# Second branch's output matrix as seven block products over all twelve K tiles, product by product, with half of the layer norm kept on chip

## The chip, the cores and the metric

The kernel runs on one core of one Trainium2 chip. The engines meant below are TensorE (PE: matmuls into PSUM; PEld is its weight load), VectorE (DVE), ScalarE (ACT), GpSimd (POOL, which here issues transfers that add into their target) and SyncE (SP, which issues plain loads and stores). Each engine works through its own list of instructions in the order of the program and waits for the others by semaphores. The metric is the time of one execution in microseconds; the median of three runs is given, lower is better.

## The reference, cut to what matters

Everything is float32; batch 1, 1024 positions, model width 1024. The part around the change:

```python
u = va * jax.nn.sigmoid(ga)
u = causal_depthwise_conv(u, conv_a_w[l], conv_a_b[l])
u = jax.nn.silu(layer_norm(u, ln_g[l], ln_b[l]))          # over 1024 channels
y_a = jnp.einsum("bsc,cd->bsd", u, w_a_out[l])            # K = 1024 = 8 tiles of 128

v = causal_depthwise_conv(xb, conv_b_w[l], conv_b_b[l])
v = rg_lru(v, w_rg_a[l], b_rg_a[l], w_rg_x[l], b_rg_x[l], lam[l])
y_b = jnp.einsum("bsc,cd->bsd", v * jax.nn.gelu(gb), w_b_out[l])   # K = 1536 = 12 tiles of 128

m = jax.nn.sigmoid(sa) * y_a + jax.nn.sigmoid(sb) * y_b
x = x + jnp.einsum("bsc,cd->bsd", m, w_o[l])
```

Ahead of it stand an RMS norm and the input projection z, behind it the MLP and two more norms. The change touches y_b and the layer norm.

## The kernel before

**Arithmetic.** A float32 matmul is made of three in the float32r type, with each factor split into a high and a low part: high by high, high by low, low by high. The high part is a copy by ACT; the low part (the factor less its high part) is made either by DVE or by `split_dma`: ACT writes the negative of the rounded value, a POOL transfer adds the factor to it, ACT writes the high part. A matmul multiplies one 128x128 tile of weights or activations with one of 128x512. Large matrix products use Strassen's scheme in Winograd's form: two by two blocks, seven block products (1 to 7) instead of eight, with sums of blocks ahead of them (s1 to s4 on the weights' side, t1 to t4 on the other) and sums of products behind them.

**Order.** The stages around the change lie in `manual_schedule`: the order on each engine is the one in which the Python code issues it. Small tables (`ZX`, `BX`, `GX`) say which preparations come after which product; `at` keeps a rough clock for each engine, and `later`, `vector_work` and the norm's generator use that clock to choose where DVE's work is put in. Buffers come from pools: 37 tiles of 128x1024 (`T`), 7 more (`W`, weights3), 15 of 128x512 (`EV`, evac3), eight PSUM banks of 128x512 (`bank`). A tile that takes a used buffer waits for that buffer's last reader; if it is a load, SP waits, and all of SP's list behind it.

**Branch b.** The gated recurrence's output lies in DRAM as `hgd`, 12 tiles of 128x1024 (channels x positions). y_b has four pairs of output tiles, i = 0 to 3. For each pair, K tiles 4, 5, 10 and 11 go through the seven products (`b_mm` with "1" to "7", 6 matmuls each), and the other eight K tiles through four plain blocks ("00", "01", "10", "11", 24 matmuls each), which add to the same banks. The weights come in two arrays, `w_b_pl` (8 x 512 KB) and `w_b_sq` (4 x 512 KB); their parts are made by ACT and DVE (`b_split`). The order is pair by pair (`bseq`). `b_post` and `b_out` multiply each finished 128x512 block by its gate sb and store it to DRAM (`mbd`).

**Layer norm.** The convolved branch a lies in DRAM as `yd`, 8 tiles. Its two halves over positions are o = 0 and 1. One generator (`n_all`) does the statistics of half 1, then of half 0, then scales both. `n_stats` subtracts the mean, squares (ACT), adds, and sums over channels by two matmuls with a constant matrix, so that the variance stands in a PSUM bank (var), the same in all 128 rows. Half 1's tiles (yc) are stored back to yd after the mean is off and loaded again for the scaling. 1/sigma is one root and a Newton step on 128x512 numbers (lv, lsd, lr: a reciprocal and four more rows on DVE).

**Behind it** comes the stage g: y_a with the same seven products, product by product (`GORD`) and i = 0 to 3 within a product, where ga1h, ga1l and so on are parts of the normed tiles q, and wa tiles are loads of w_a_out; then the product with w_o.

Of the kernel before, what the change touches and what calls it, by code (L numbers as in the profile page):

```python
# [9 lines left out]
F32 = mybir.dt.float32  # L10
# [20 lines left out]
def trunk_kernel(ctx: ExitStack, tc: tile.TileContext, x, xt_in, xt_eo, vecs, w_in, w_a_out, w_b_pl, w_b_sq,  # L31
# [1003 lines left out]

    ZX = {0: ((x_parts, 1, 7),), 2: ((x_parts, 1, 5),), 4: ((x_parts, 1, 4),)}
    H_AT = {2: (0, 0), 5: (1, 1), 3: (0, 1), 4: (1, 0)}
    with tc.manual_schedule(engines=ENGINES):

        hg, hraw, hb_, hbo, wraw_, wop = {}, {}, {}, {}, {}, {}  # L1040

        def hg_load(*ts):
            for t in ts:
                hraw[t] = T(f"hg{t}")
                nc.sync.dma_start(hraw[t], hgd[t])

        def b_split(a, name, mk, mk2=None):
            h, l = mk(name + "h", F32R), (mk2 or mk)(name + "l", F32R)
            nc.scalar.activation(h, a, AF.Copy)
            later(at("A", 1.0), 1.2, nc.vector.tensor_tensor, l, a, h.bitcast(F32), ALU.subtract)  # L1050
            return h, l

        def hg_parts(*ts):
            for t in ts:
                hg[t] = b_split(hraw.pop(t), f"hg{t}", X1 if t == 9 else T)

        def hb_load(kk, hf):
            hb_[kk, hf] = a = T(f"hb{kk}{hf}")
            for c in range(2):
                nc.sync.dma_start(a[:, HALVES[c]], hgd[4 + c + 6 * kk, :, HALVES[hf]])  # L1060

        def hb_t(*ns):

            if 2 in ns:
                hb_[2] = T("hbt2")
            for n in ns:
                o, a, b = {1: ((0, 0), (0, 1), (0, 0)), 2: (2, (1, 1), (0, 0)),
                           3: ((0, 1), (1, 1), (0, 1)), 4: ((1, 0), (1, 0), 2)}[n]
                later(0, 1.2, nc.vector.tensor_tensor, hb_[o], hb_[a], hb_[b], ALU.subtract)

        def hb_parts(p):
            b = {1: (0, 0), 5: (0, 0), 2: (1, 0), 4: (1, 0), 3: (1, 1), 7: (0, 1), 6: 2}[p]
            hbo[p] = b_split(hb_[b], f"hb{p}", T)

        def a_load(i):
            if i < 4:
                wraw_[i, "a"] = a = (W if i else T)(f"wba{i}")
                nc.sync.dma_start(a, w_b_sq[i])

        def a_sums(i):  # L1080
            if i < 4:
                a, s = wraw_[i, "a"], T(f"wbs{i}")
                wraw_[i, "s"] = s
                a11, a12, a21, a22 = (a[:, n * 2 * P:(n + 1) * 2 * P] for n in range(4))
                s1, s2, s3, s4 = (s[:, n * 2 * P:(n + 1) * 2 * P] for n in range(4))
                for o, x, y, op_ in ((s1, a21, a22, ALU.add), (s2, s1, a11, ALU.subtract),
                                     (s3, a11, a21, ALU.subtract), (s4, a12, s2, ALU.subtract)):
                    later(0, 0.4, nc.vector.tensor_tensor, o, x, y, op_)

        def a_parts(i, x):  # L1090
            if i < 4:
                wop[i, x] = b_split(wraw_.pop((i, x)), f"wb{x}{i}", T, W if i and x == "a" else T)

        def p_load(j):
            if j < 8:
                wraw_[j, "p"] = a = (W if j else T)(f"wbp{j}")
                nc.sync.dma_start(a, w_b_pl[j])

        def p_parts(j):
            if j < 8:  # L1100
                wop[j, "p"] = b_split(wraw_.pop((j, "p")), f"wbp{j}", W if j else T)
# [16 lines left out]
        def b_mm(i, x):  # L1118
            if len(x) == 1:
                p = int(x)  # L1120
                b = {1: "b", 2: "a", 3: "e", 4: "b", 5: "e", 6: "b", 7: "f"}[p]
                if p in (1, 7):
                    yb_[i, b] = bank(f"yb{i}{b}")
# [1171 lines left out]
```

## Time and profile before

| | |
|---|---|
| Median of 3 runs | 1528.11 us (1528.05 to 1528.63) |
| Profiled execution | 1528.49 us, span of the records 1526.7 us |
| Branch-b stage, first matmul to the first of stage g | 624.20 to 751.24 us |
| PE, DVE, ACT, POOL busy over the span | 99%, 79%, 61%, 12% |
| Granted TensorE clock | 0.999 |

A row of the profile's timeline gives start and length in us, engine, source line, operation, output tile and input tiles, partitions x elements, a count if rows were put together, and in brackets the idle time before it with what ended that. Lengths of neighbours on one engine overlap, so the cost of one in a row of many is the distance from start to start. PE busy at 99% says that some matmul was always under way.

### The profile page before, as it was taken

The page shows a single profiled execution, that of the slowest core. Times are in us where ns is not written, and L with a number is a line of the kernel's source. Part 1 is how long each engine was busy: PE and PEld are TensorE (multiplying, and loading weights), DVE is VectorE, ACT ScalarE, POOL GpSimd, SP SyncE. Part 2 cuts the span into 40 slices and gives each one's busy share as a digit, 9 for nine tenths or more (in the row PEclk, how much of TensorE's full clock was granted, in tenths as well). Part 3 has the DMA queues.
Part 4 walks back from the last instruction along what each step waited for, and adds up shares of the span by engine and source line. Part 5 has one row for each costly group of instructions (what it writes and reads, how often), then busy time and mean ns, then how long its engine had stood idle before and what let it go on. Part 6 is the DMA issues. An engine that isn't in the chain of part 4 may idle for free.

```text
span 1526.7 us, 18955 instructions
## 1 busy us (share of the span) xinstructions
PE 1517.1 (99%) x6712; PEld 1248.3 (82%) x6712; DVE 1200.7 (79%) x1640; ACT 928.1 (61%) x1299; POOL 190.7 (12%) x228
## 2 busy tenths in 40 slices
PE   9999999999999999999999999999999999999998
PEld 7878887888888888888888888888888888888886
DVE  6999996999999997788769879755555387777777
ACT  6748688576566667645475777554444455545475
POOL 0111011022222222000022322000000000101010
PEclk9999999999999999999999999999999999999999
DMA  8757778698997789964779897333333974776464
GB/s 352 192 135 165 178 179 187 199 262 211 266 254 179 182 207 277 304 216 120 268 197 302 191 213 174 124 127 111 111 111 111 308 264 125 181 206 171 106 124 152
DMA packets 130911, 295.48 MB, mean 194 GB/s; under 512 B 12800, under 2 KB 34944, under 8 KB 130816
## 3 DMA queue, kind: packets, MB, share of 16 engines
q1 hardware_dynamic: 98960, 214.83, 41.5%
q0 software_dynamic: 31568, 78.92, 27.4%
q8 instruction: 52, 0.85, 0.2%
q10 hardware_dynamic: 288, 0.52, 0.1%
q14 instruction: 43, 0.35, 0.1%
HBM read 148.74 MB, written 60.82 MB: 137 GB/s over the span
## 4 chain that ended last, share of the span: by engine, by line
PE 99%; DMA 0%; DVE 0%; ACT 0%; SPq 0%; issue 0%
PE z L743 16%; PE d2b L2015 2%; PE d1b L2015 2%; PE d0b L2015 2%; PE z L273 2%; PE d3b L2015 2%; PE d0e L2015 1%; PE d3e L2015 1%; PE d3a L2015 1%; PE d2e L2015 1%; PE d1e L2015 1%; PE d1a L2015 1%; PE d0a L2015 1%; PE d2a L2015 1%; PE rg L550 1%; PE rg L552 1%
## 5 line engine op out<-in xcount | busy, mean ns | idle before, releaser
L743 PE MATMUL z<-xh,win_h 128*128 128x512 f32 x368 | 115.4, 391 | 0.0
L743 PE MATMUL z<-xl,win_h 128*128 128x512 f32 x368 | 114.9, 390 | 0.0
L655 DVE SCALAR_TENSOR_TENSOR y<-u,vec,y 128x511 f32<-128x511 f32 (+14 forms) x120 | 88.7, 739 | 0.0
L743 PE MATMUL z<-xh,win_l 128*128 128x512 f32 x368 | 87.5, 389 | 0.0
L655 DVE SCALAR_TENSOR_TENSOR yt<-u,vec,yt 128x511 f32<-128x511 f32 (+6 forms) x112 | 82.9, 740 | 0.0
L655 DVE SCALAR_TENSOR_TENSOR y<-yt,csum,y 128x511 f32<-128x511 f32 (+6 forms) x112 | 82.9, 740 | 0.0
L743 PEld LDWEIGHTS z<-xh,win_h 128*128 128x128 f32 x368 | 69.1, 188 | 16.0 <-ACT win_h L67 0.4
L743 PEld LDWEIGHTS z<-xl,win_h 128*128 128x128 f32 x368 | 69.1, 188 | 14.9
L743 PEld LDWEIGHTS z<-xh,win_l 128*128 128x128 f32 x368 | 69.1, 188 | 14.6
L560 ACT ACTIVATE g<-rg,vec 96x1024 f32<-96x1024 f32 x32 | 35.5, 1111 | 72.7 <-PE rg L552 72.7
L1710 ACT ACTIVATE o<-s 128x512 fp32r<-128x512 f32 x56 | 33.8, 624 | 45.2 <-DVE s L1694 26.4
L66 POOL DMA_DIRECT2D zo<-zw x45 | 38.9, 864 | 133.7 <-ACT zo L65 118.4
L501 DVE SCALAR_TENSOR_TENSOR v<-xb,vec,v 128x1023 f32<-128x1023 f32 (+2 forms) x36 | 46.2, 1282 | 4.4 <-ACT v L492 3.5
L66 POOL DMA_DIRECT2D db_10l<-br x4 | 3.5, 868 | 338.3 <-DMA br<-in_w_dram 253.1
L66 POOL DMA_DIRECT2D win_l<-win_raw x23 | 19.8, 861 | 190.6 <-ACT win_l L65 161.9
L65 ACT ACTIVATE zo<-zw 128x512 fp32r<-128x512 f32 x45 | 28.2, 627 | 24.3 <-PE z10f L944 2.1
L1234 DVE TENSOR_TENSOR o<-s,o 128x512 fp32r<-128x512 f32 x56 | 37.3, 684 | 1.5 <-ACT o L1710 1.5
L66 POOL DMA_DIRECT2D zo<-zs x30 | 26.1, 871 | 75.8 <-ACT zo L65 63.8
L67 ACT ACTIVATE zo<-zw 128x512 fp32r<-128x512 f32 x45 | 28.0, 622 | 0.0
L596 DVE TENSOR_TENSOR_SCAN g<-a,g 128x1024 f32<-128x1024 f32 x12 | 27.5, 2292 | 0.4
L66 POOL DMA_DIRECT2D ga<-gsa x8 | 6.9, 866 | 161.2 <-DMA m<-mbd 150.9
L1234 DVE TENSOR_TENSOR o<-w_raw,o 128x512 fp32r<-128x512 f32 x38 | 25.9, 685 | 0.0
(3178 smaller groups left out, 4908.2 us busy)
## 6 DMA issues: line engine op xcount, KB each, us to landing
w_raw<-in_w_dram SPq DMA_DIRECT2D x32, 512.0 KB, 5.5
br<-in_w_dram SPq DMA_DIRECT2D x32, 512.0 KB, 5.6
ar<-fd SPq DMA_DIRECT2D x32, 512.0 KB, 6.9
zw<-in_w_in_dram SPq DMA_DIRECT2D x28, 512.0 KB, 6.9
win_raw<-in_w_in_dram SPq DMA_DIRECT2D x23, 512.0 KB, 4.8
win_l<-win_raw POOLq DMA_DIRECT2D x23, 512.0 KB, 5.1
zo<-zw POOLq DMA_DIRECT2D x45, 256.0 KB, 5.7
gates<-zg SPq DMA_DIRECT2D x32, 256.0 KB, 4.5
```

The lines of the kernel that those rows point to most:

```text
L65: nc.scalar.activation(l, src, AF.Copy, scale=-1.0)
L66: nc.gpsimd.dma_start(l, src, accum_op=ALU.add)
L67: nc.scalar.activation(h, src, AF.Copy)
L273: nc.tensor.matmul(z0[i][:, HALVES[hf]], w0[i][w][:, k, :], xpart(a, hf, k), start=k == 0 and which == "hh", stop=k == 7 and which == ("hl ...
L501: nc.vector.scalar_tensor_tensor(v[:, d:S], a[:, 0:S - d], cbw_c[:, w * 12 + t:w * 12 + t + 1], v[:, d:S], ALU.mult, ALU.add)
L560: nc.scalar.activation(a, gps.pop((n, gi))[:HD, :], AF.Sigmoid, bias=(ba_c, bx_c)[gi][:, n:n + 1])
L596: nc.vector.tensor_tensor_scan(i, a, i, 0.0, ALU.mult, ALU.add)
L655: nc.vector.scalar_tensor_tensor(o[:, k:], a[:, 0:HS - k], c, o[:, k:], ALU.mult, add)
L743: nc.tensor.matmul(zps[s][:, HALVES[hf]], w[:, k, :], xw[k][part][hf], start=n == 0, stop=n == 23)
L1234: tt(l, src, h.bitcast(F32), ALU.subtract)
L1710: nc.scalar.activation(o[:, 0], src, AF.Copy)
L2015: nc.tensor.matmul(o, a, b, start=start and n == 0, stop=stop and n == len(todo) - 1, skip_group_check=not start or not stop)
```

## The change

1. y_b: all 12 K tiles go through the seven block products. A block is six K tiles by 128 or 512 columns, so a product of one pair is 18 matmuls. The order is product by product, 1, 2, 6, 7, 4, 5, 3, with i = 0 to 3 in each: 28 steps, numbered from 0 (`bsq`). The weights are one array; a block of it is a 128x768 tile (wb{i}{block}), loaded seven steps ahead (`bl_get`), summed five steps ahead on DVE (`b_sums`, where needed), split four steps ahead (`b_lhs`): products 1, 2 and 4 by ACT and DVE, products 6, 7, 5 and 3 by `split_dma`. The other side (hb) has 21 split tiles of 128x1024 and 12 sums.
2. Layer norm: half 1 stays in eight `EV` tiles (yc) from its load to its scaling; nothing is stored back or loaded again. Each half has a generator of its own. The mean is copied from PSUM (`mean_mm`).
3. 1/sigma: the variance's diagonals are taken out of the PSUM bank by four 128x128 rows on DVE with an accumulated output (lj, lnst), so that root and Newton step work on 128x4. The result is spread again: four diagonal 128x128 tiles, high part by ACT (ldh) and low part by DVE (ldl), and two matmuls with ones into a bank (rs).
4. `g_mm` is moved up and serves both stages; the table `BX` is written anew.

The diff, cut to its core:

```diff
-        def b_split(a, name, mk, mk2=None):
...
-        PLAIN = (0, 1, 2, 3, 6, 7, 8, 9)
-        bseq = [(0, "1")]
-        for i in range(4):
-            bseq += [(i, x) for x in ("7", "6", "00", "5", "2", "4", "01", "3", "10")]
-            bseq += [(i + 1, "1")] * (i < 3) + [(i, "11")]
...
+    bsq = [(i, p) for p in GORD for i in range(GP)]
+    def g_mm(w, i, p):
+        b = {1: "a", 2: "a", 6: "b", 5: "e", 3: "e", 7: "f", 4: "f"}[p]
+        if w == "b" and p in (7, 4):
+            b = "b"
+        if p in (1, 5):
+            gb[w, i, b] = bank(f"g{w}{i}{b}")
...
+        nk = 6 if w == "b" else 4
+        for k in range(nk):
+            h, l = (a[w, p, k // 2][:, HALVES[k % 2]] for a in (gh, gl))
+            for a, b_ in ((oh[:, k, :], h), (oh[:, k, :], l), (ol[:, k, :], h)):
+                nc.tensor.matmul(gb[w, i, b], a, b_, start=p in (1, 5) and n == 0, stop=n == 3 * nk - 1,
...
+        LB = {1: (11,), 2: (12,), 6: (21, 22, 11), 7: (), 4: (22,), 5: (), 3: (12,)}
...
+            if p == 6:
+                ws[i] = wr[i, 22]
+                op(ws[i], wr[i, 21], wr[i, 22], ALU.add)
+                op(wr[i, 21], wr[i, 11], wr[i, 21])
+                op(wr[i, 11], ws[i], wr[i, 11])
+            elif p == 3:
+                op(wr[i, 12], wr[i, 12], wr[i, 11])
...
+            if p in BY_V:
+                nc.scalar.activation(h, a, AF.Copy)
+                later(at("A", 0.8), 0.9, nc.vector.tensor_tensor, l, a, h.bitcast(F32), ALU.subtract)
+            else:
+                split_dma(a, h, l)
...
+        def b_step(n):
+            i, p = bsq[n]
+            if n:
+                b_post(n - 1)
+            b_gate(n + 2)
+            g_mm("b", i, p)
+            b_lhs(n + 4)
+            b_sums(n + 5)
+            if n != 1:
+                for k in range(8 if n == 2 else n + 7, n + 8):
+                    bl_get(k)
...
-        v, s, r = EV(f"lv{o}"), EV(f"lsd{o}"), EV(f"lr{o}")
-        nc.vector.tensor_scalar(v, pv, EPS, None, ALU.add)
+        for b in range(4):
+            d = slice(b * P, b * P + P)
+            nc.vector.scalar_tensor_tensor(junk[:, d], pv[:, d], 1.0, ident, ALU.mult, ALU.mult,
+                                           accum_out=cv[:, b:b + 1])
+        nc.vector.tensor_scalar(v, cv, EPS, None, ALU.add)
         nc.scalar.activation(s, v, AF.Sqrt)
...
+        newton_rstd(r, v, s, t, False)
+        dh, dl = (vp.tile([P, HS], F32R, tag="ev", name=f"ld{x}{o}") for x in "hl")
+        for b in range(4):
+            d = slice(b * P, b * P + P)
+            nc.scalar.activation(dh[:, d], ident, AF.Copy, scale=r[:, b:b + 1])
+            nc.vector.scalar_tensor_tensor(dl[:, d], ident, r[:, b:b + 1], dh[:, d].bitcast(F32),
+                                           ALU.mult, ALU.subtract)
...
+        rstd[o] = ps = bank(f"rs{o}")
+        for k, d in enumerate((dh, dl)):
+            nc.tensor.matmul(ps, ones.bitcast(F32R), d, start=k == 0, stop=k == 1)
...
-    norm = n_all()
+    norms = [n_half(1), n_half(0)]
...
+          23: ((n_to, 0, 4), (g_parts, "a", 1, 0), (g_parts, "a", 1, 1), (g_load, "a", 2, 0)),
+          24: ((g_load, "a", 3, 0),), 25: ((n_to, 0, 8), (n_to, 1, 8), (g_t, "a", 0, 1, 2), (g_t, "a", 1, 1, 2)),
```

`n_to(o, n)` runs half o's generator until n of its tiles are scaled, whatever the clocks say.

Three places in the order of instructions (the number behind a tile's name only tells equal names apart).

TensorE, around the variance of half 0, now: the last matmuls of step 23 (product 5, i = 3, bank gb3e), and the first of step 24.

```order
L1052 MATMUL gb3e_6284<-hb5l2_6120,wo3_5h_6153 128x512
L1052 MATMUL gb3e_6284<-hb5h2_6119,wo3_5l_6154 128x512
L1282 MATMUL var0_6308<-var0h_6128,onesm_78 128x512
L1283 MATMUL var0_6308<-var0l_6129,onesm_78 128x512
L1360 MATMUL rs0_6333<-ldh0_6323,ones_69 128x512
L1360 MATMUL rs0_6333<-ldl0_6324,ones_69 128x512
L1052 MATMUL gb0e_6165<-hb3h0_6191,wo0_3h_6184 128x512
```

Before, the same variance stood between two products of pair 2:

```order
L1144 MATMUL yb2a_5891<-hb2l_5365,wba2h_5812 128x512
L1144 MATMUL yb2a_5891<-hb2h_5364,wba2l_5813 128x512
L1259 MATMUL var0_6021<-var0h_5998,onesm_78 128x512
L1260 MATMUL var0_6021<-var0l_5999,onesm_78 128x512
L1144 MATMUL yb2b_5875<-hb4h_5469,wba2h_5812 128x512
L1144 MATMUL yb2b_5875<-hb4l_5470,wba2h_5812 128x512
```

The rs0 pair is new, and reads what ACT and DVE make out of var0; it stands with no other product between. In all TensorE has 5806 rows now and had 5850.

DVE, now, on the way from the variance of half 0 into the last steps and the first of stage g (rows for half 1 and for gates among them; behind the last row shown come the g_t sums and four more pairs like gbu0 and sb01):

```order
L1340 SCALAR_TENSOR_TENSOR lj0_6311,lnst0_5448<-var0_6308,ident_73 128x128 x4
L1342 TENSOR_SCALAR lnst0_5448<-lnst0_5448 128x4
...
L1352 SCALAR_TENSOR_TENSOR ldl0_6324<-ident_73,lnst0_5448,ldh0_6323 128x128 x4
L1371 TENSOR_TENSOR q000_5720<-q000_5720,rs0_6333 128x512 x2
L1371 TENSOR_TENSOR q001_5723<-q001_5723,rs0_6333 128x512 x2
...
L1256 TENSOR_TENSOR ga0_1_6379<-wa0_0_6237,ga0_1_6379 128x512
L1371 TENSOR_TENSOR q100_5726<-q100_5726,rs0_6333 128x512 x2
L1371 TENSOR_TENSOR q101_5729<-q101_5729,rs0_6333 128x512 x2
...
L480 TENSOR_TENSOR gbu0_5738<-gbu0_5738,gb0e_6165 128x512
L1153 TENSOR_TENSOR sb01_6246<-gbu0_5738,sb01_6246 128x512
```

Before, ahead of stage g:

```order
L1153 TENSOR_TENSOR sb70_6307<-ybc3_6367,sb70_6307 128x512
L1234 TENSOR_TENSOR ga2l0_6393<-q100_5600,ga2h0_6392 128x1024
L1234 TENSOR_TENSOR ga2l1_6396<-q101_5603,ga2h1_6395 128x1024
L480 TENSOR_TENSOR ybf3_6199<-yb3g_6251,ybf3_6199 128x512
L1153 TENSOR_TENSOR sb71_6309<-ybf3_6199,sb71_6309 128x512
L480 TENSOR_TENSOR q100_5600<-q100_5600,gt2a0_6327 128x1024
L1234 TENSOR_TENSOR ga0_2_6418<-wa0_1_6363,ga0_2_6418 128x512
```

The scalings of half 0 stood far ahead of this place before; now all of them, and four of half 1's, come after rs0, with the last products' sums and gates between.

SP, now, from step 2 on: loads of the blocks for product 6 (21, 22 and 11 of each pair), of the norm's half 1 and of gates.

```order
L1201 DMA sb00_5456<-gates_2797 128x2x256
L1095 DMA wb021_5480<-in_w_b_dram 128x768
L1095 DMA wb022_5482<-in_w_b_dram 128x768
L1095 DMA wb011_5484<-in_w_b_dram 128x768
L1095 DMA wb121_5486<-in_w_b_dram 128x768
...
L1293 DMA yc000_5496<-yd_430 128x512
...
L1095 DMA wb311_5590<-in_w_b_dram 128x768
L1201 DMA sb60_5599<-gates_2797 128x2x256
L1154 DMA mbd_5447<-sb00_5456 256x1x256
```

wb021 takes the buffer of a left part of step 2 (wo2_1h), so its load waits until TensorE has done step 2; the 22 rows behind it up to sb60 follow on the same queue. Before, no load of the stage stood in such a group: weights came as one 512 KB tile after another.

More of the change, by code (lines that the diff above doesn't have):

```diff
@@ L1071, in hb_parts @@
[L1071 to L1088, printed above, removed]
```

360 lines of the change are left out of this document (171 added, 189 removed).

## The prediction

> **What bounds the kernel now.** I read the page first (busy shares, then the chain that ended last), then TensorE's waits, then the stretches around the changed stage, then single rows. From the page:
>
> ```profile
> span 1526.7 us, 18955 instructions
> ...
> PE 1517.1 (99%) x6712; PEld 1248.3 (82%) x6712; DVE 1200.7 (79%) x1640; ACT 928.1 (61%) x1299; POOL 190.7 (12%) x228
> ...
> PE 99%; DMA 0%; DVE 0%; ACT 0%; SPq 0%; issue 0%
> ```
>
> TensorE's waits, all that the profile has:
>
> ```profile
> PE z L273 <- ACT xh L235: 1.3, 1, 1.3
> PE spare L360 <- POOL ones L108: 1.0, 1, 1.0
> ```
>
> So TensorE is the only bound, and after the first 7 us it never waits. Each matmul taken out is worth its whole pitch, and each wait put in front of TensorE costs its whole length. The branch-b stage in the view by stretches (columns: length, then busy time and count of PE, PEld, DVE, ACT, POOL, then clock, DMA share, GB/s), its first two pieces, and the first 19 us of the a-branch stage behind it:
>
> ```profile
> core 0: us, PE busy (x) PEld busy (x) DVE busy (x) ACT busy (x) POOL busy (x), PEclk, DMA share, GB/s
> 624.20:751.24 127.04, 127.04 (x561) 105.11 (x560) 99.94 (x131) 63.83 (x87) 0.00 (x0) 1.00 0.62 206
> 624.20:640.00 15.80, 15.80 (x71) 13.11 (x70) 14.00 (x17) 12.24 (x16) 0.00 (x0) 1.00 0.86 295
> 640.00:655.50 15.50, 15.50 (x70) 12.80 (x69) 9.53 (x14) 4.12 (x7) 0.00 (x0) 1.00 0.86 283
> ...
> 751.24:770.00 18.76, 18.76 (x84) 15.56 (x83) 18.28 (x24) 8.23 (x15) 1.95 (x3) 1.00 0.87 277
> ```
>
> A matmul costs 127.04 / 561 = 0.2265 us here. The second reading is the one that matters: DVE has 27 us of room in the stage, and none just behind it (18.28 of 18.76 us).
>
> **Part 1, matmuls.** Before, each of four output pairs takes 7 products of 6 matmuls and 4 plain blocks of 24: 4 x 138 = 552. After, 28 steps of 18: 504. The means and variances keep 8 matmuls, and the two new spreads of 1/sigma bring 4. Net -44 x 0.2265 = **-9.97 us**, all of it on the bound. One step is 18 x 0.2265 = 4.08 us.
>
> **Part 2, DVE's load.** The prices per DVE instruction (start to start), and what stands at the end of the stage:
>
> ```profile
> 732.40 0.69 DVE L1153 TENSOR_TENSOR sb<-yb3a,sb 128x512 f32<-128x512 f32 x1 [4.52 <-PE yb3a L1144]
> 733.01 1.28 DVE L1328 TENSOR_TENSOR q<-q,lr 128x512 f32<-128x512 f32 x2
> 734.21 2.35 DVE L1234 TENSOR_TENSOR ga1l<-q,ga1h 128x1024 fp32r<-128x1024 f32 x2
> ...
> 741.48 1.22 DVE L480 TENSOR_TENSOR q<-q,q 128x1024 f32<-128x1024 f32 x1
> 742.80 1.23 DVE L480 TENSOR_TENSOR gt2a<-q,q 128x1024 f32<-128x1024 f32 x1
> 743.94 1.29 DVE L1234 TENSOR_TENSOR ga<-wa,ga 128x512 fp32r<-128x512 f32 x2
> ...
> 751.44 0.69 DVE L480 TENSOR_TENSOR ybf<-yb3g,ybf 128x512 f32<-128x512 f32 x1 [1.47 <-PE yb3g L1144]
> 752.17 0.69 DVE L1153 TENSOR_TENSOR sb<-ybf,sb 128x512 f32<-128x512 f32 x1
> 752.78 1.22 DVE L480 TENSOR_TENSOR q<-q,gt2a 128x1024 f32<-128x1024 f32 x1
> ...
> 779.00 0.69 DVE L1234 TENSOR_TENSOR ga<-wa,ga 128x512 fp32r<-128x512 f32 x1
> ...
> 782.25 1.23 DVE L1234 TENSOR_TENSOR ga4l<-q,ga4h 128x1024 fp32r<-128x1024 f32 x1 [0.16 <-ACT ga4h L1384]
> ```
>
> ```profile
> 666.47 0.42 DVE L480 TENSOR_TENSOR wbs<-wba 128x256 f32<-128x256 f32 x1
> 666.81 0.42 DVE L480 TENSOR_TENSOR wbs<-wba,wbs 128x256 f32<-128x256 f32 x1
> ...
> 670.39 3.35 DVE L98 RECIPROCAL lr<-lsd 128x512 f32<-128x512 f32 x1 [0.70 <-ACT lsd L1314]
> ```
>
> A 128x512 sum takes 0.60 (733.01 to 734.21 is two), a 128x1024 1.14 (1.32 when the next one reads it), a dependent pair sum and gate (751.44 to 752.78) 1.34, a 128x256 0.34. A 128x768 isn't in the trace; between 0.60 and 1.14 I take 0.87. In the order of instructions, from the last z14 row to the row before g's first step, DVE had 83 of 512 columns, 28 of 1024, 12 of 256 and two reciprocals; now it has 78 of 512, 32 of 1024, 24 of 768, 16 of 128 and a few of 4 columns: 78 x 0.62 + 32 x 1.14 + 24 x 0.87 + 16 x 0.3 + 12 x 0.2 = 113 us (0.62 since some depend on each other; by the same prices before's come to 97, where 99.94 were measured), in a TensorE stage that shrinks to 516 x 0.2265 = 117. DVE goes from 79% to 97% of the stage, so any wait of DVE's in it becomes lateness. There are three places.
>
> **Place 1, steps 3 to 8: the lower blocks.** At the start of step 3 SP is held at the load of wb021, whose buffer is free only at the end of step 2; 22 more loads (7.2 MB: 11 blocks, the 8 yc tiles, 3 gates) stand behind it. DVE's sums of step 3 wait for its landing, with everything of DVE's behind them. How long loads took in the stage (last figure, median us to landing):
>
> ```profile
> wba<-in_w_b_sq_dram SPq DMA_DIRECT2D x3, 512.0 KB, 5.2
> ga<-gsa POOLq DMA_DIRECT2D x3, 256.0 KB, 3.2
> hb<-hgd SPq DMA_DIRECT2D x2, 256.0 KB, 8.9
> ```
>
> From the end of step 2: landing and two issues 6.2, 12 block sums 12 x 0.87 = 10.4 with 0.8 for dependence, 3 hb sums 3.4, a 768 split 0.9, hb6l0 and hb6l1 2.3, two gates 1.3, hb6l2 1.2: 26.5 us. TensorE reads hb6l2 as the third K group of step 8, at 5 x 4.08 + 0.45 (the mean's two matmuls) + 12 x 0.2265 = 23.6. So **+2.5 us** or so (26.5 - 23.6 = 2.9, some of it given back where a load lands early); bounds 0 (768 columns at 0.62) and 6.5 (8.9 us to land, as hb).
>
> **Place 2, step 23: var0 and rs0.** The two rs0 matmuls stand directly behind the two of var0. TensorE must wait there for a whole chain: four 128x128 sums out of PSUM, an add, the root on ACT, five Newton steps, four diagonal copies, their low parts. Before, a variance went into the row of matmuls with the next product behind it:
>
> ```profile
> 668.43 0.39 PE L1260 MATMUL var<-var1l,onesm 128*128 128x512 f32 x1
> 668.66 0.40 PE L1144 MATMUL yb1b<-hb4h,wba1h 128*128 128x512 f32 x1
> ```
>
> The handover: the last yb3g matmul, and DVE's 751.44 above, 0.43 after it.
>
> ```profile
> 751.01 0.39 PE L1144 MATMUL yb3g<-hg9h,wbp7l 128*128 128x512 f32 x1
> 751.24 0.39 PE L1440 MATMUL ga0a<-ga1h,ga 128*128 128x512 f32 x1
> ```
>
> The rest from the RMS norm's small chain on DVE, and on ACT:
>
> ```profile
> 889.18 0.13 DVE L1613 TENSOR_SCALAR stm<-cs 128x4 f32<-128x4 f32 x1
> ...
> 889.83 0.17 DVE L98 RECIPROCAL stm<-stm 128x4 f32<-128x4 f32 x1
> ...
> 890.82 0.48 DVE L1625 TENSOR_SCALAR rdm<-ident,stm 128x128 f32<-128x128 f32 x2
> ```
>
> ```profile
> 889.35 0.21 ACT L1614 ACTIVATE stm<-stm 128x4 f32<-128x4 f32 x1 [3.58 <-DVE stm L1613]
> ...
> 890.82 0.70 ACT L1627 ACTIVATE rdm<-ident,stm 128x128 f32<-128x128 f32 x2 [0.22 <-DVE stm L105]
> 891.42 0.62 ACT L65 ACTIVATE go<-wo 128x512 fp32r<-128x512 f32 x1
> ```
>
> Handover 0.43; four sums of 128x128 4 x 0.30 = 1.2 (between 0.24, of 890.82's pair, and 0.34, of 256 columns); add to root 0.17; root 0.25; Newton 889.83 to 890.82 = 0.99; four copies at 0.60 / 2 = 1.2 and 0.1 for the last; its low part 0.25; 0.05 to TensorE: 4.64. Less the pitch that is counted anyway, 0.23: **+4.4 us**, bounds 3.5 and 6. ACT is free there: by the order its last work before is a block of step 27's left side (wo3_3), two passes that can start early in step 23. The first norm (var1 in step 14, rs1 in step 18) has steps between and costs nothing.
>
> TensorE idle for 4.4 us also asks what its clock does. The trace has only the start, 20 small matmuls and an idle of 1.26 us:
>
> ```profile
> 1.00 3.93 PE L360 MATMUL spare<-ones 128*128 128x128 f32 x20 [1.00 <-POOL ones L108]
> 6.19 0.50 PE L273 MATMUL z<-xh,w_h 128*128 128x512 f32 x1 [1.26 <-ACT xh L235]
> ```
>
> I put 0 for it, since every stretch shown has a granted 1.00. The Trainium skill, "TensorE: Matmul & The Clock Gate", Part 1 (The HAM clock gate), says otherwise: an idle window of about 3.4 us takes the clock to half, and a busy window as long is needed to get it back; 3.4 us at half rate would be an estimated 1.7 us lost, and the sum 1531.3. No row here shows it.
>
> **Place 3, steps 24 to g: DVE's queue.** From rs0's first matmul (T0) DVE has, before g's first step's row (752.78's counterpart): 12 scalings x 0.60 = 7.2, six pairs of sum and gate x 1.34 = 8.0, four ga low parts x 0.60 = 2.4, four ga1l/ga2l x 1.14 = 4.6, four g_t sums 2 x 1.32 + 2 x 1.14 = 4.9: 27.1 us. TensorE reaches g after 2 + 72 matmuls, 74 x 0.2265 = 16.8; before, DVE stood 752.78 - 751.24 = 1.54 behind. So DVE enters g 27.1 - 16.8 - 1.5 = 8.8 us later than before. From there its rows are the same as before's, and before it ran from 751.44 to 782.25 without a gap over 0.2 us, so it can't catch up. What TensorE has in hand there, in the tightest place I found (ga0_7, the row at 779.00, done 779.69):
>
> ```profile
> 783.88 0.39 PE L1440 MATMUL ga0f<-ga7h,ga 128*128 128x512 f32 x1
> ```
>
> is 4.2 us. **+4.6 us** (8.8 - 4.2); bounds 3.4 (pairs and g_t sums at the price of independent rows, 1.2 less) and 8.8 (no slack).
>
> **Costed at nothing.** 16 more POOL transfers in the stage: POOL did nothing there (0.00), and each is issued four steps (16 us) ahead of its use against 3.2 us to land; without that cover each would be its 3.2. Loads: 28 x 384 KB against 12 x 512 KB is 4.5 MB more, 16 x 256 KB of norm writes and reloads are 4 MB less, so DMA stays near 0.62. The big Newton steps (670.39 and four more, twice) go from DVE, where they held up nothing. ACT splits 28 left blocks, 16 of them in two passes, and six right tiles more: at DVE's prices 44 x 0.87 + 6 x 1.14 against 16 x 1.14, 27 us more than 63.8, so 91 of 117. SP's stores of gated tiles wait for DVE's late gates, with g's wa loads behind them; by the rows they still land 1 to 2 us before DVE wants them.
>
> **Sum.** -9.97 + 2.5 + 4.4 + 4.6 = +1.5 on the profiled execution's 1528.49 (span 1526.7 and 1.8 around it), which stands 0.38 above the median of 1528.11: **1529.6 us** on the runs' basis. What this kernel's runs can tell from no change is about 0.2%, 3.06 us, so this is "no change".
>
> **Rivals.**
> A, DVE catches up (0.19). Places 1 and 3 cost nothing because DVE's queue runs shorter than my pitches; only the chain at step 23 is left: 1528.1 - 10.0 + 4.4 = 1522.5. For it: DVE had gaps like the 4.52 at 732.40. Against: after, 113 of 117 us are booked.
> B, all of it hidden (0.10): 1518.1. It needs rs0 not to wait, and the order has nothing between.
> C, slower by late loads (0.16). At place 1 each load lands as hb's 8.9 and not 5.2, 3.7 us more, and the 7.2 MB behind it, at the stage's 206 GB/s, need 35 us and not the 22 that the sums leave: 1529.6 + 4 to 6 = 1534.5. It decides the sign once place 1 costs over 4.1 us (2.5 + 1.6). For it: the DMA share of 0.86 in the stage's first 31 us. Against: 295 and 283 GB/s were carried there.
> D, slower by the clock (0.09). After place 2's idle TensorE runs at double pitch for as long as the opening row lasted, 3.93 us, so loses half of it: 1529.6 + 2.0 = 1531.6, just over the bound. Against: no granted clock under 1.00 in any stretch, though none has such an idle. The Trainium skill's clock gate page, cited above, would have it so.
> E, slower in g (0.09). None of the 4.2 us of slack is there since ACT and POOL's accumulations follow DVE: 1529.6 + 4.2 = 1533.8.
> That the change doesn't do what it says is out: the order has 5806 rows on TensorE against 5850.
>
> **Chances.** The forecast 0.37, its own range 1525 to 1531; A and B, faster, 0.29 with 0.02 of the forecast's edge, so 0.31; C, D, E, slower, 0.34; within 0.2%, 0.35. The range leaves out B (0.10) and the far end of C and E (0.08), so 1520 to 1536.
>
> **What would show it.** Right: 44 matmuls fewer; TensorE's only new waits in three places (step 8 on DVE's hb6l, rs0 of about 4.4 us, g's first 16 steps on DVE), 11 to 12 us in all; DVE busy over 95% from step 24 to ga0f. Wrong: rs0's wait under 2 us, no wait in g, a granted clock below 1.00 in the stretch behind rs0, or a wait of TensorE's for a POOL transfer.

## The result, and the profile after

The median after is 1555.21 us (four runs, 1554.26 to 1557.26), before it is 1528.22 us: ratio 1.0178, interval 1.016 to 1.0196. That is 27 us slower, where 1529.6 us was forecast with a range to 1536. The profiled execution took 1557.26 us, 28.8 above that of before. Its page, in the same places as before's:

```profile
span 1555.3 us, 19018 instructions
...
PE 1520.0 (98%) x6668; PEld 1245.4 (80%) x6668; DVE 1210.3 (78%) x1674; ACT 953.3 (61%) x1341; POOL 204.0 (13%) x244
...
PE 85%; issue 6%; DMA 4%; DVE 2%; ACT 1%; POOL 0%; POOLq 0%; ACTq 0%; SPq 0%; DVEq 0%
```

TensorE has the 44 matmuls less (6712 to 6668), but the chain that ended last, 99% TensorE's before, is TensorE's for 85% of the span only. TensorE's waits of over 1 us from 600 us on, where before had none (columns: who waits for whom, us in total, times, longest):

```profile
PE gb0b L1052 <- DVE hb6l L480: 6.6, 1, 6.6
PE rs L1360 <- ACT ldh L1351: 4.9, 1, 4.9
PE ga0f L1052 <- DMA ga<-wa: 3.8, 1, 3.8
PE gb0e L1052 <- DVE hb5l L480: 2.4, 1, 2.4
PE z14e L944 <- ACT zc L1021: 2.4, 1, 2.4
PE z14f L944 <- DVE zc L480: 1.8, 1, 1.8
PE gb0b L1052 <- DVE hb7l L480: 1.6, 1, 1.6
```

Added up row by row from 590 to 1000 us, TensorE idles 26.2 us, and loses 12.2 us more to matmuls at a slow pitch behind such waits (the pitch is the time from one matmul's start to the next one's; slow is 0.43 us instead of 0.227): -10.0 + 26.2 + 12.2 = +28.4, against 28.8 between the two profiled executions. Of these, 25.1 us have come together when TensorE takes up ga0f behind its last long wait (820.37 us; the same matmul of before stands at 795.22), and 3.4 come behind it. The slow pitch at the wait on rs0, in TensorE's timeline:

```profile
744.56 0.39 PE L1283 MATMUL var<-var0l,onesm 128*128 128x512 f32 x1
749.87 0.51 PE L1360 MATMUL rs<-ldh,ones 128*128 128x512 f32 x1 [4.92 <-ACT ldh L1351]
750.26 0.80 PE L1360 MATMUL rs<-ldl,ones 128*128 128x512 f32 x1
750.85 0.63 PE L1052 MATMUL gb0e<-hb3h,wo_3h 128*128 128x512 f32 x1
751.28 0.63 PE L1052 MATMUL gb0e<-hb3l,wo_3h 128*128 128x512 f32 x1
...
753.76 0.40 PE L1052 MATMUL gb0e<-hb3l,wo_3h 128*128 128x512 f32 x1
754.00 0.39 PE L1052 MATMUL gb0e<-hb3h,wo_3l 128*128 128x512 f32 x1
```

Starts are 0.43 us apart up to 753.4, then 0.23. The granted clock over 750 to 760 us is 0.83.

What the other engines waited for. First ACT at step 0, and then SP's queue, in which the load that ACT waited for stands behind six hb loads:

```profile
617.80 0.85 ACT L1130 ACTIVATE wo_1h<-wb 128x768 fp32r<-128x768 f32 x1 [5.78 <-DMA wb<-in_w_b_dram]
```

```profile
605.20 2.88 SPq L1068 DMA_DIRECT2D hb<-hgd  x6
608.84 1.35 SPq L1095 DMA_DIRECT2D wb<-in_w_b_dram  x2
```

ACT's zc, which TensorE's z14e wants, stood behind that row. Then DVE ahead of step 8:

```profile
667.16 0.96 DVE L480 TENSOR_TENSOR wb<-wb,wb 128x768 f32<-128x768 f32 x1 [3.06 <-DMA wb<-in_w_b_dram]
670.26 1.95 DVE L480 TENSOR_TENSOR wb<-wb,wb 128x768 f32<-128x768 f32 x2 [2.15 <-DMA wb<-in_w_b_dram]
672.13 1.22 DVE L480 TENSOR_TENSOR hb6l<-hbt,hb6h 128x1024 fp32r<-128x1024 f32 x1
```

Two block loads cost DVE 5.2 us there, and hb6l stands behind the sums. Both are of the last pair. The loads of the first two pairs' blocks and those of the last pair's, in SP's queue:

```profile
642.83 2.71 SPq L1095 DMA_DIRECT2D wb<-in_w_b_dram  x6
...
656.13 4.07 SPq L1095 DMA_DIRECT2D wb<-in_w_b_dram  x3
```

The first six landed 3.2 to 6.5 us after their issue, the last three after 9.1 to 10.3 us. The queues in the stage (620 to 751 us; packets, MB, share of the time of the 16 DMA engines; then issues with their median us to landing), before:

```profile
q1 hardware_dynamic: 17733, 27.60, 63.3%
...
mbd<-sb SPq DMA_DIRECT2D x15, 256.0 KB, 2.5
```

and after:

```profile
q1 hardware_dynamic: 15881, 25.17, 54.2%
q0 software_dynamic: 2183, 5.97, 24.9%
...
wb<-in_w_b_dram SPq DMA_DIRECT2D x24, 384.0 KB, 6.1
...
mbd<-sb SPq DMA_DIRECT2D x10, 256.0 KB, 7.3
...
wo_6l<-wb POOLq DMA_DIRECT2D x4, 384.0 KB, 7.6
```

POOL's accumulating transfers (q0) are a quarter of the DMA engines' time. Per MB they take 24.9 / 5.97 = 4.2% of it, loads and stores 54.2 / 25.17 = 2.2%. A store of a gated tile lands after 7.3 us instead of 2.5.

The stage from its first matmul to the first of stage g, which the prediction put at 117 us (columns as in its view by stretches):

```profile
630.39:768.51 138.12, 122.60 (x518) 99.64 (x516) 104.63 (x160) 89.99 (x128) 13.80 (x16) 0.96 0.75 218
```

DVE is busy for 104.6 of these 138.1 us and ACT for 90.0.

### The profile page after: what moved, and what is told of

Its sections match the earlier page's. It is cut to its first block, busy times and chain, and to the rows that moved or that the text cites. A ratio compares the mean times of both kernels' runs of the same rounds, so it can differ in the third digit from the quotient of the medians.

```text
span 1555.3 us, 19018 instructions
## 1 busy us (share of the span) xinstructions
PE 1520.0 (98%) x6668; PEld 1245.4 (80%) x6668; DVE 1210.3 (78%) x1674; ACT 953.3 (61%) x1341; POOL 204.0 (13%) x244
## 4 chain that ended last, share of the span: by engine, by line
PE 85%; issue 6%; DMA 4%; DVE 2%; ACT 1%; POOL 0%; POOLq 0%; ACTq 0%; SPq 0%; DVEq 0%
PE z L743 16%; PE z L273 2%; PE d2b L2033 2%; PE d1b L2033 2%; PE d0b L2033 2%; PE d3b L2033 2%; PE d0e L2033 1%; PE d3e L2033 1%; PE d3a L2033 1%; PE d2e L2033 1%; PE d2a L2033 1%; PE d1a L2033 1%; PE d0a L2033 1%; PE d1e L2033 1%; DMA wb<-in_w_b_dram 1%
## 5 line engine op out<-in xcount | busy, mean ns | idle before, releaser
L480 DVE TENSOR_TENSOR zo<-zs,zo 128x512 fp32r<-128x512 f32 x30 | 20.5, 685 | 4.6 <-ACT zo L788 4.6
```

## The experiments

In all of them "wait + slow" is a wait of TensorE and the time lost by slow pitch behind it, both in us and both from the one profiled execution, the second to about 0.2 us. The runs of a version, four or more, are up to 5.4 us apart, so a difference of 2 us between two medians shows little. Before, run beside each group, had medians of 1528.1 to 1529.0 us.

**One repair at a time.** A fill of the wait at rs0:

```diff
         pv = n_mm(f"var{o}")
+        rsb = bank(f"rs{o}") if not o else None
+        for _ in range(0 if o else 18):
+            nc.tensor.matmul(rsb, ones.bitcast(F32R), gh["b", 3, 0][:, HALVES[0]], start=True, stop=True)
```

> The changed kernel with 18 throw-away matmuls (128x512, into the bank that rs0 overwrites) between var0 and rs0, so that TensorE works through 4.1 of the 5.1 us for which it stood still; nothing else differs. Clock theory (an idle of over 3 us makes TensorE's matmuls take 0.43 instead of 0.227 us for the next 4 us): the matmuls behind rs0 stand 0.227 apart and the run is about 2 us faster than the changed kernel, so 1553. Rival (the slow matmuls there come from something else, such as DMA traffic or ACT's table load): they stay 0.43 apart for 9 matmuls, 1555. The idle time before rs0 falls to about 1 us in both.

Measured: 1555.06 us (1552.27 to 1557.64). The wait on rs0 shrank to 0.79 with 0.53 lost behind it (4.92 and 2.0 in the change), so the slow pitch there did come from the idle. The median did not move, but with 5.4 us between the four runs the 2 us of theory and rival cannot be told apart by it.

The chain from var0 to rs0 spread over steps 20 to 23 (`n_ph` runs half 0's generator to its next stop):

```diff
-          20: ((hb_parts, 3, 0), ...), 21: ((hb_parts, 3, 1), ...), 22: ..., 23: ((n_to, 0, 4), ...
+          20: ((n_ph, 0, 1), (hb_parts, 3, 0), ...), 21: ((n_ph, 0, 2), ...), 22: ((n_ph, 0, 3), ...), 23: ((n_ph, 0, 4), (n_to, 0, 4), ...
```

> The changed kernel with half 0's chain pulled apart: var0's matmuls behind step 20, the diagonals and the root in step 21, the Newton step and the diagonal tiles in step 22, rs0's matmuls behind step 23 as before. Theory (the wait is the chain's length, and what it costs is the wait and the slow clock after it): the wait for rs0 goes, 4.9 + 2.0 us less, so 1548, and stage g keeps its waits of about 6 us. Rival (DVE is simply late, and the chain's time comes back in stage g or as a wait for var0): 1552 or more.

Measured: 1554.41 us (1553.52 to 1555.64). rs0: 1.28 + 0.6. In stage g a new wait on ga1a, 3.03 + 1.9: what was won at rs0 was given back 20 us later.

The blocks of steps 1 to 3 loaded ahead of the hb tiles:

```diff
-L - 8: ((hb_parts, 1, 2), (bl_get, 1), (hb_load, 1, 0)), L - 7: ((b_lhs, 0), (bl_get, 2)), L - 6: ((b_lhs, 1), (bl_get, 3)),
+L - 8: ((hb_parts, 1, 2), (bl_get, 1), (bl_get, 2), (bl_get, 3), (hb_load, 1, 0)), L - 7: ((b_lhs, 0),), L - 6: ((b_lhs, 1),),
```

> The changed kernel with the two loads of block 11 for i = 2 and 3 put on SP's queue ahead of the six loads of hb10 instead of behind them. Theory (ACT stands 5.8 us at the split of a block that lands late, with z's copies behind it, so TensorE waits 2.4 and 1.8 us for z14e and z14f and then runs at the slow clock for 1.6 us): those waits go, 4 to 6 us less, about 1550. Rival (the transfers are simply too many for the DMA engines there, whatever the order): the wait moves to hb2's parts or to the next blocks, and the time stays within 2 us of 1555.

Measured: 1555.22 us (1554.46 to 1557.42). ACT no longer waits, but now the hb loads are the late ones: DVE waits 3.81 us for them, and z14f waits 4.19 + 2.5.

The eight yc loads moved from steps 2 and 3 to steps 5 and 6:

```diff
-    BX = {2: ((hb_t, 4), (mean_parts, 1), (n_ahead, 4)), 3: ((hb_t, 3), (mean_mm, 1), (n_ahead, 4)),
+    BX = {2: ((hb_t, 4), (mean_parts, 1)), 3: ((hb_t, 3),),
...
+          5: ((hb_parts, 6, 1), (n_ahead, 4)), 6: ((hb_parts, 6, 2), (n_ahead, 4), (mean_mm, 1)),
```

> The changed kernel with the eight loads of half 1 of the norm (2 MB) moved from steps 2 and 3 to steps 5 and 6, behind the loads of the last lower blocks; the mean of half 1 is multiplied in step 6. Theory (place 1's wait of 6.6 us and the 2.5 us of slow clock behind it come from blocks that land late because 7 MB stand in the queue): blocks for i = 2 and 3 land some 5 us earlier and the wait for hb6l shrinks to under 3 us, with no slow clock: 6 to 9 us less, 1547 to 1549. Rival (SP is held by buffers, or DVE's own 26 us of work decides): less than 2 us gained, 1554.

Measured: 1551.92 us (1549.93 to 1552.58). hb6l waits 0.71 us instead of 6.58 + 2.7, so the queue of loads was its cause. The time fell by 3.3 us only: 5 us came back as waits on hb7h and hb7l, behind ACT's wo_7l, which waited 4.74 us for a buffer that a POOL transfer was still reading.

**Repairs together.** First e3's edit with `(hb_t, 1)` moved from L - 3 to L + 1, so that z14 no longer stands behind the hb loads:

> As the run with the two blocks loaded ahead of hb10, and the sums hb01 - hb00 (needed only for product 6, at step 8) moved from ahead of z14's last sum on DVE to behind step 1. Theory (whatever on ACT or DVE waits for a late load ahead of z14's copies holds TensorE): both z14 waits go, with the slow clock after them, 6 us less than the changed kernel: 1549. Rival (the transfers themselves are too late for hb2 or the blocks of product 2): a wait of 3 us or more turns up within steps 0 to 7, and the time stays above 1552.

Measured: 1560.06 us (1558.75 to 1560.92). The z14 waits are gone and step 20 comes 6 us earlier, but rs0 waits 13.31 + 2.5: its first DVE row (lj) waited 9.01 us for an EV buffer whose store (mbd) had not landed. All this time came back at 750 us.

Then f1, e4's and e2's edits and the q loads at step 10 instead of 8:

> All repairs of order in one: the blocks first, hb01's sums later, half 1's loads in steps 5 and 6, half 0's loads in step 10, var0's chain pulled apart over steps 20 to 23. Theory (each place is a late row in a queue that works in order, and the places are independent): 6 + 8 + 6 us less, 1535 to 1537, with stage g's waits left. Rival (there is too little time on DVE and too few buffers, so a repaired place shows up again further on): at least half of it comes back, 1543 or more.

Measured: 1546.05 us (1545.66 to 1547.63), ratio 1.0115 (1.01 to 1.013): 9 us of the 27 are order. What is left: mu (the mean's matmuls) 5.20, hb5l 2.52, ga1a 5.42 + 3.0, ga0f 3.88 + 1.9.

f1 with lj in a 128x128 tile of its own:

> As the run with hb01's sums later, and the throw-away output of the four diagonal sums (lj) in a 128x128 tile of its own instead of in one of the 15 EV buffers. Theory (there rs0 waited 13.3 us because lj's buffer was still being stored to DRAM as a gate tile; eight of the 15 are held by the kept half): the wait for rs0 falls back to the chain's 5 us, 8 us less, 1551 or 1552. Rival (DVE and ACT reach that point at about 750 us whatever TensorE does): it stays over 10, 1558 or more.

Measured: 1557.78 us (1557.36 to 1558.04). lj waits no more, and rs0 still waits 10.53 + 2.1: the next taker of an EV buffer, ACT's ldh, now waited 7.42 us for the next store.

f2 with that tile, and the mean's matmuls at step 8:

> As the run with all repairs of order, with lj in a tile of its own and the mean of half 1 multiplied in step 8 instead of 6 (there it waited 5.2 us for a bank and 1.9 us of slow clock followed). Theory: 7 us less than that run, 1539; stage g's waits (about 10 us, with 5.6 of slow clock) stay. Rival (the time comes back at the next place): 1544 or more.

Measured: 1546.52 us (1544.63 to 1548.11), as f2. rs0 and mu are gone, the wait moved to hb6l (twice 2.6), hb5l 2.43, ga1a 4.61, ga0f 3.53.

Part 2 of the change undone: half 1 stored back and loaded again (`yd` store behind the mean, scaling on q):

> The changed kernel with the layer norm's half 1 stored back and loaded again as in the kernel before (the rest of the change stays): undoes the keeping on chip. Theory (the eight EV buffers held by the kept half make rows wait for stores: var0h for 2.5 us, and so hb5l and TensorE for 2.4): that wait goes, 2 us less; the places ahead of step 12 stay as they were; 1553. Rival (4 MB more of transfers cost more than the buffers give): 1556 or more.

Measured: 1561.72 us (1560.07 to 1562.56), 6.5 us worse than the change: hb6l 7.87 + 2.3, rs0 12.35 + 1.9. DVE waits 9.35 us there for a tile that is loaded again. In this order, keeping half 1 on chip helps.

**DVE's load.** The 16 multiplications by 1/sigma left out:

```diff
-            tt(a, a, rstd[o], ALU.mult)
```

> The changed kernel without the 16 multiplications of the normed tiles by 1/sigma (left out of the computation); rs0's matmuls stay and still wait for the chain. Theory (stage g waits because DVE has 27 us of rows between rs0 and g where TensorE has 17): 12 rows of 0.6 fewer there, DVE enters g 7 us earlier and g's waits (5.9 us and 2.2 us of slow clock) shrink to under 2: 6 to 8 us less, 1548. Rival (g's waits come from the POOL transfers and loads of wa, not from DVE): they stay, 1553 or more. The wait for rs0 stays at 4.9 in both.

Measured: 1554.41 us (1553.2 to 1556.78). In stage g every wait on DVE is gone; only ga0f, 2.00 + 2.0, is left of 5.9 and some 4. So DVE's queue made place 3, except for some 2 us on ga0f. But rs0 now waits 8.42 + 2.7, and the total stays: ACT, which no scaling holds back, does half 1's eight activations (from 735.46 us, 5.76 long) ahead of hb3h, and DVE waits 6.07 us for that.

f2 with the low parts of stage g's products 1, 2 and 7, and of y_b's product 4, made by POOL transfers instead of DVE (`p in ()`, `BY_V = (1, 2)`):

> As the run with all repairs of order, and besides, the low parts of the left sides of stage g's products 1, 2 and 7 and of y_b's product 4 made by ACT and POOL transfers instead of by DVE (12 x 0.6 and 4 x 0.87 = 10.7 us off DVE, 16 more transfers). Theory (DVE's 113 of 117 us is what lets every lateness stay): g's waits for DVE go, 4 to 8 us less than the run with the repairs alone, near 1530. Rival (ACT or the transfers' landing takes DVE's place): no gain over that run.

Measured: 1553.52 us (1552.8 to 1554.36), 7.5 us worse than f2. In stage g TensorE now waits for transfers:

```profile
PE ga2a L1052 <- DMA ga<-wa: 4.6, 1, 4.6
PE ga1a L1052 <- DMA ga<-wa: 3.9, 1, 3.9
```

f2 with all of the layer norm's arithmetic left out (no mean, no variance, no scaling; before had that arithmetic too), half 1 loaded straight into q:

> As the run with all repairs of order, without the layer norm's arithmetic (mean, variance, scaling left out; the convolved tiles go through the activation and on, both halves loaded straight into place): the seven products over twelve K tiles by themselves, with the loads repaired. It takes 46 rows of 0.6 us, the chain and the eight kept EV buffers away. Theory (DVE and its buffers don't hold product part and norm together in 117 us): the waits of steps 8 to 27 and most of stage g's go, 1520 to 1526, below the kernel before. Rival (the blocks' loads and POOL transfers alone are too much): 1532 or more.

Measured: 1531.32 us (1530.21 to 1533.94), ratio 1.0023 (1.0013 to 1.0032). Even alone the block products gain nothing: this version has 56 matmuls fewer than before (6656; 48 of y_b's and the norm's 8), 12.7 us, and 7.8 us of waits and 5.75 of slow pitch eat that. DVE, busy 131 of the 200 us from 600 us on, is not full there, so something else was late too.

**The clock.** A 128x64 weight tile of zeros, multiplied into the waiting bank so that TensorE is busy ahead of a wait (counts by product, pair and row):

```diff
+                for _ in range(FILL.get((w, i, p, n), 0)):
+                    nc.tensor.matmul(gb[w, i, b][:ZW], zero.bitcast(F32R), gh[w, p, 0][:, HALVES[0]], start=False,
+                                     stop=False, skip_group_check=True)
                 nc.tensor.matmul(gb[w, i, b], a, b_, start=p in (1, 5) and n == 0, ...
```

> The changed kernel with throw-away matmuls (a zero weight tile, adding nothing to the same bank) ahead of five of TensorE's waits, so that it is busy while it waits: 24 ahead of the hb6l wait of step 8 (5.4 of 6.58 us), 8 and 12 ahead of those on hb7l and hb5l, 18 ahead of rs0, 16 ahead of ga0f. No other engine gets or loses a row that matters. Theory 1, the slow clock behind a wait is time of its own: the 2.7 + 0.3 + 0.3 + 2.0 + 2.9 us of slow pitch behind these five go, 6 to 8 us in all, and the time falls from 1555.2 to about 1548. Theory 2, the late engine alone sets the end (what TensorE wins behind one wait it loses at the next, as in the run with rs0 alone filled): the pitch behind the five is 0.227, and the time stays at 1554 to 1556, with longer idles or fillers in their place.

Measured: 1555.88 us (1555.62 to 1560.22). Ahead of hb6l stand the 24 throw-away matmuls, and behind it the pitch is now full:

```profile
664.86 5.67 PE L1057 MATMUL gb0b<-hb6h,zero 128*64 128x512 f32 x24
671.94 0.50 PE L1059 MATMUL gb0b<-hb6l,wo_6h 128*128 128x512 f32 x1 [1.40 <-DVE hb6l L480]
672.27 0.39 PE L1059 MATMUL gb0b<-hb6h,wo_6l 128*128 128x512 f32 x1
672.50 0.40 PE L1059 MATMUL gb0b<-hb6h,wo_6h 128*128 128x512 f32 x1
```

Idle fell from 26.2 to 13.3 and slow pitch from 12.2 to 6.8; the 78 throw-away matmuls are 17.7 us. 13.3 + 6.8 + 17.7 = 37.8 against 38.4: conserved, and theory 2 holds. It is not that these matmuls held TensorE up themselves: at hb6l and rs0 it still waited behind them (1.40 and 3.05 us), and at hb7l, hb5l and ga0f they outlasted the wait by less than 0.5 us.

> The version with all repairs of order (1546.5 us, TensorE idle 17.6 us and 10.1 us of slow pitch) with the same throw-away matmuls ahead of its six longest waits: 10 and 10 ahead of the two on hb6l, 11 on hb5l, 19 on ga1a, 6 on ga0b, 15 on ga0f. Theory 1, the slow clock is time of its own: 8 us or so go, 1538 to 1540. Theory 2, the late engine sets the end: 1545 to 1548.

Measured: 1547.15 us (1546.19 to 1548.02) against g3's 1546.52: theory 2 again. 6.5 idle, 4.7 slow, 71 throw-away matmuls at 16.1: 27.3 against g3's 27.7. Up to ga1a every one of them ended ahead of what it waited for, 2.2 us of slow pitch were gone, and ga1a came at 762.40 us as in g3 (762.22). Behind it they were too many: at ga0b they outlasted the wait by 0.9 us, and ga0f's tile landed at 810.8 us and was taken at 813.01. So on the last 2 us this run says nothing.

> The version that leaves out the layer norm's arithmetic (1531.3 us; idle 7.8 us and 5.75 of slow pitch) with 9, 9 and 8 throw-away matmuls ahead of its three longest waits (hb6l twice, hb3h). DVE has room in this version, so a wait is not pushed on. Theory 1 (clock is time of its own): 4 to 5 us go, 1526.5, faster than the kernel before. Theory 2 (given back at the next wait): 1530 to 1532.

Measured: 1532.78 us (1530.74 to 1535.22) against g4's 1531.32: nothing gained; a wait of 3.45 + 1.9 on ga0f (0.72 in g4) took it.

**The transfers.** The 16 POOL accumulations of the stage cut to 16 of 128 rows, so that seven eighths of these low parts are left out; every instruction stays:

```diff
-                split_dma(a, h, l)
+                nc.scalar.activation(l, a, AF.Copy, scale=-1.0)
+                nc.gpsimd.dma_start(l[:16], a[:16], accum_op=ALU.add)
+                nc.scalar.activation(h, a, AF.Copy)
```

> The changed kernel, with the sixteen POOL transfers that make low parts in the stage (products 6, 7, 5 and 3) cut to 16 of their 128 rows, so that seven eighths of these low parts are left out; ACT's two passes, their order and every other row stay. In the changed kernel these transfers are 5.97 MB in POOL's queue and take 24.9% of the sixteen DMA engines from 620 to 751 us, where the kernel before had none. Theory 1, the transfers are the overlooked load (loads, stores and ACT's left parts land late because the DMA engines are full): the waits on hb6l, hb7l and of ACT for landing tiles shrink, and the time falls by 8 us or more, to 1547 or less. Theory 2, DVE and ACT's rows and the order of loads set the end and the transfers lie beside them: 1553 to 1556.

Measured: 1545.25 us (1543.85 to 1548.22), ratio 1.0114 (1.0098 to 1.0129): 10 us less than the change, which is theory 1. The stage's queues, 620 to 751 us:

```profile
q1 hardware_dynamic: 17281, 26.96, 60.1%
q0 software_dynamic: 512, 0.79, 6.0%
...
mbd<-sb SPq DMA_DIRECT2D x12, 256.0 KB, 4.3
```

and TensorE's waits:

```profile
PE rs L1362 <- ACT ldh L1353: 4.9, 1, 4.9
PE ga0f L1052 <- DMA ga<-wa: 2.8, 1, 2.8
PE z14e L944 <- ACT zc L1021: 2.3, 1, 2.3
PE gb0b L1052 <- DVE hb6l L480: 2.2, 1, 2.2
```

Stores and gates land earlier, and the blocks a little (6.1 to 5.8 at the median), hb6l waits 2.2 and not 6.6, and rs0 comes at 738.99 instead of 749.87: 10.9 us are won before it. About 2 of these lie between any two executions: this one starts step 4 at 645.32 instead of 647.39 us, ahead of the first cut transfer (649.56). A cut transfer also gives back its buffer earlier (ACT's wait for wo_7l falls from 2.5 to 0.8 us), so the run shows what the transfers cost, and not how much of it is the DMA engines' time.

> The version with all repairs of order (1546.5 us) with the same cut of the sixteen transfers to 16 rows. Theory 1 (DMA engines full): 1540 or less. Theory 2 (DVE and ACT's rows): 1545 to 1547, since its waits on hb6l, hb5l and ga1a are DVE's.

Measured: 1545.55 us (1542.91 to 1547.52) against 1546.52: theory 2. The better order had already taken what the transfers cost; the two repairs remove the same lateness, and don't add. Most of what is left are waits on DVE:

```profile
PE ga1a L1052 <- DVE ga L1258: 5.4, 1, 5.4
PE gb0b L1052 <- DVE hb6l L480: 5.2, 2, 2.6
```

> The version without the layer norm's arithmetic (1531.3 us, DMA share 0.80 to 1.06 in every 25 us from 600 to 750) with the same cut. DVE has room here. Theory 1: most of its 13.5 us of waits and slow pitch go, 1520 to 1524, faster than the kernel before. Theory 2 (order of loads and the chain between ACT and DVE): 1529 to 1532.

Measured: 1525.44 us (1522.41 to 1526.8), ratio 0.9979 (0.997 to 0.9988): 5.9 us less than g4, between the theories (1520 to 1524, 1529 to 1532). With the norm's arithmetic and seven eighths of the transfers both left out, the time is 2.7 us under before's. The norm's 8 matmuls of before account for 1.8 of these (8 x 0.2265), so of the 10.9 us of y_b's 48 matmuls less than 1 is left. No version that computes everything came near the kernel before; the best is f2 at 1546.05.

## Why the prediction was wrong, by its own steps

- **Part 1, 44 matmuls, -9.97.** Right in count and pitch. The step that failed is what was done with it: "each wait put in front of TensorE costs its whole length" adds up waits as if TensorE stayed the bound. From 617 to 820 us it is not: in h1 and h2 half of the slow pitch was gone, and what TensorE won it waited at the next place (rs0 in h1, ga1a in h2). There the end is set by loads, ACT and DVE, and a saving on TensorE is worth nothing.
- **Costed at nothing: POOL's transfers and the loads.** This is the worst term. "DMA stays near 0.62" counted loads and stores in MB and left out the 16 accumulations, 5.97 MB at twice the engines' time per MB. The share rose to 79% (54.2 + 24.9), each transfer took 5.9 to 7.6 us where 3.2 was taken from a smaller one in an emptier stretch, and g's wa loads, which were to land "1 to 2 us before DVE wants them", kept ACT waiting for 8.5 us in all. i1 measures the term: about 10 us in the change as it is. The Trainium skill, "DMA: Bandwidth & Descriptors", Issuing engines are not separate DMA queues, says that DMAs run on the same 16 engines whichever engine started them; i1 agrees (with POOL's transfers cut, SP's gated-tile stores land after 4.3 and not 7.3 us).
- **Not seen: ACT at step 0.** ACT's split of a late block held zc for z14e, 2.4 us, and DVE's zc for z14f, 1.8 + 1.9. The stage's loads begin before its first matmul, in a stretch (600 to 625 us) where the DMA share was 1.07 already before the change, and the prediction began at step 3.
- **Place 1, +2.5, bounds 0 and 6.5.** Measured 6.58 + 2.7. The place, the tile and the queue were right, and e4 confirms the queue. The row in it was not: wb021 landed 3.2 us after its issue, and DVE waited 0.35 us for the first blocks. The sum took one landing of 5.2 us and then unbroken DVE work; the last pair's blocks took 9.1 to 10.3 us, as rival C had it, and cost DVE 5.2 us.
- **Place 2, +4.4, bounds 3.5 and 6.** Measured 4.92. Right, also in its cause: e2 takes it away. But f1 and g1 show what it lacked: buffers of EV, eight of fifteen held by yc, come free only with a store, and in an earlier order that makes it 10 to 13 us.
- **Place 3, +4.6, bounds 3.4 and 8.8.** Measured 5.9 of idle, 3.8 of it on ga0f. DVE needed 27.3 us from 751.09 to 778.39, where the 27.1 was forecast; f3 confirms DVE for most of it. The slack of 4.2 us was read at a row of DVE's. The tightest place was a POOL transfer: in before, ga0f's low part was issued at 786.50, landed 7.3 us later and was read at 795.22, a slack of 1.4 us. Now it was issued at 812.10 and took 8.2 us. DVE's timeline, the first and last rows of the 27.3 us and the next row that waited:

```profile
751.09 2.48 DVE L1371 TENSOR_TENSOR q<-q,rs 128x512 f32<-128x512 f32 x4 [0.89 <-PE rs L1360]
...
778.39 1.22 DVE L480 TENSOR_TENSOR q<-q,gt2a 128x1024 f32<-128x1024 f32 x1
...
816.35 1.23 DVE L1256 TENSOR_TENSOR ga5l<-q,ga5h 128x1024 fp32r<-128x1024 f32 x1 [4.81 <-ACT ga5h L1421]
```

- **The clock, 0, and rival D, +2.0.** The slow pitch came as D said, 2.0 us behind rs0 and 12.2 in all. That it costs time at rs0 fell: with half of it filled away in h1 and h2, the time was the same, since TensorE waits again soon. Behind the last long wait it does cost: from ga0f to the end of the span e1 and e3, with hardly any slow pitch there, take 731.6 us, e2, e4, f1, f2 and g1, with 1.7 us of it, 733.2 to 733.7, and the change, with 2.4, takes 734.9. The Trainium skill's page "TensorE: Matmul & The Clock Gate", Part 1, gives the half rate after an idle window; the rows agree (0.43 for 0.23).
- **DVE at 97% of the stage.** It was 76%: 104.6 us of rows in 138.1. The booked 113 us were not far off, since the last of these rows ran behind the stage's end, up to 778.39 (before's rows, by the prices listed, add up to 94 us and not to the 97 given). But the stage grew with the waits. DVE is full only in stretches, as behind rs0 (26.7 of the 27.3 us); elsewhere it waits for ACT and for loads.
- **Rivals.** C was nearest: late loads, but at more places and with the transfers as a large part of their cause. A and B, the faster ones, needed DVE to have room, and f3 and g4 show what happens then: the next late thing is ACT, a load or a transfer. Two of the prediction's own signs of being wrong came: a granted clock of 0.83 behind rs0, and a wait of TensorE's for a POOL transfer (ga0f).

So of 27 us, about 10 are the transfers' (i1) or, in another order, 9 the order's (f2), and not both. The rest goes away with the norm's arithmetic: 1545.55 (i2) to 1525.44 (i3). That is an upper bound, since before had most of that arithmetic as well, and leaving it out also takes 12 matmuls, the chain to rs0 and the eight kept buffers. TensorE's waits in i2 name DVE for 11.6 of 16.3 us, though DVE is busy only 102 of that stage's 128 us. Open is how the 17 us divide between DVE and ACT: they wait for each other all along the stage, and no run separated them. Also untested are the order product by product by itself and the small 1/sigma (part 3) by itself.

## What to carry to other kernels

When the shorter stage would leave another engine only 3% of room, ask first whether the bound changes hands; if it does, the terms are no longer added on the first engine, and repairs of single waits only show where the next one is. Count DMA engines' time and not MB: an accumulating transfer took twice a load's per MB. To test whether a slow clock behind waits costs time, put useless work into the waits, less than they are long: if the slow pitch goes and the time stays, repair something else.

## What the runs showed of the hardware

- Which idles slow TensorE, over the 145 waits of 0.5 us or more from 600 to 1000 us in the changed kernel and the eighteen experiments: of 68 under 1.76 us, one is followed by over 1 us of slow pitch (0.75 us, 1.3 us behind another wait of 2.05); of 50 from 1.76 to 3.44 us, 26 lose over 1.5 us and 24 less than 1; and all 27 above lose 1.5 to 3.2. A wait of 2.42 us on hb5l lost 0.29 us in the change, and one of 2.43 us lost 1.9 in g3. The same page of the Trainium skill calls the window of about 3.4 us free-running. That an idle's place in it decides would fit these rows, but no run sets that place. By its table it takes at least one idle window to slow the clock, and the forecast read it as a threshold; the 26 shorter idles show that it is not one.
- With the DMA share of 620 to 751 us at 0.79, the median store of a gated tile landed after 7.3 us, where before had 2.5 at 0.63. The median load of a block took 6.1 us (5.3 in i3), but the last three ahead of step 8 took 9.1 to 10.3.
